# Sixteen of the 384 densely computed tokens go to the gathered side, and the one-hots are made in a new order

## The chip, the cores and the metric

One core of one Trainium2 chip runs one launch of the kernel. The metric is the device time of that launch in microseconds. Engines are named as in the profile: PE is TensorE (matmuls), PEld its weight loads, DVE is VectorE, ACT is ScalarE, POOL is GpSimd, SP is SyncE, which only issues transfers.

## The reference

A decoder layer for 512 tokens of width 2048, all in f32: a modulated norm, one projection, eight heads of differential attention beside four heads of an mLSTM, an output projection, then the PEER layer and a last modulated norm. The change touches the PEER layer only:

```
q = (ht @ w_pq).reshape(T, PEER_HEADS, 2, PEER_QDIM // 2)      # 8 heads
s = jnp.einsum('thcd,hcnd->thcn', q, sub_keys)                 # 128 keys a side
s_top, i_top = lax.top_k(s, PEER_TOPK)                         # 16
...
idx = jnp.take_along_axis(cand_idx, pos, axis=-1)              # one of 128 x 128 experts
g = jax.nn.softmax(sc, axis=-1)
...
u_sel = jnp.take(peer_u, idx_b, axis=0)
a = jax.nn.gelu(jnp.einsum('td,thkd->thk', h_b, u_sel), approximate=False)
w = g_b * a
v_sel = jnp.take(peer_v, idx_b, axis=0)
return jnp.einsum('thk,thkd->td', w, v_sel)
```

So each token uses 8 x 16 = 128 of the 16384 experts; an expert is a row of `peer_u` and a row of `peer_v`, 2048 numbers each.

## The kernel before

The activations stand transposed, features on the partitions, tokens along the free dimension. The PEER layer is computed in two ways. For the first 384 tokens (`TD`) all 16384 experts are multiplied densely, and a table of gates, zero for experts that a token did not choose, weights the results. For the last 128 tokens the chosen rows are gathered from memory: one gather (`gather_load`) fetches one row for each of the 128 tokens, 1 MB, and `gather_use` takes it on VectorE. The rows of `peer_u` are multiplied with `h2row` and summed into one gate column `ga`; the rows of `peer_v` are added with that weight into the same tile. There are 128 gathers of `u` and 128 of `v`, in two buffers `gb`.

An f32 product on TensorE is made of three matmuls of rounded halves (`mm3`, L109 to L111: high by high, high by low, low by high). The halves come from `split`: ScalarE copies the high part (`wh`, L118), VectorE subtracts the low part (`wl`, L119). `s_pump` keeps the splits one tile ahead of their use.

The order of the work is that of the code on each engine; a wait of one instruction holds those behind it.

1. Routing. While VectorE works through the top-k (about 1020 to 1240 us), TensorE is fed with halves of u slices: a u slice is 128 experts times 384 tokens, 48 matmuls; `lead_half` computes half of one, 24 matmuls into `ps_ax`. The first 36 slices (72 halves) are made ahead of the dense stage and stored (`leadd`).
2. The loop of the gate table (about 1250 to 1580 us). `g_hot` makes, for 4 tokens, one-hots of the chosen keys: `ohj` and `ohe` by comparison on VectorE, `ohi` by products with the gates, `ohd` as a reordered copy of `ohj` on ScalarE. `g_mm` multiplies them in 12 bf16 matmuls (L1325) and ScalarE copies the result to `Gs`. Each turn has two `g_hot`, one `lead_half`, in every second turn a gather, the two `g_mm` of the turn before, and one split. 384 tokens make 96 `g_hot`, 48 turns. Behind the loop the rest of the 72 halves follows.
3. The dense stage, 256 steps. Each step takes a tile of `peer_v` (`vr`, split by ScalarE into `hh` at L1442 and by VectorE or POOL into `hl` at L1443), multiplies it with the weighted gates `Wh`, `Wl` in 24 matmuls (`ps_mm`), and adds the sum to `yT`. In steps 0 to 62 that is all TensorE does, since the u slices are ready (`ga` is loaded back); there POOL makes every second `hl`. In steps 63 to 246 a u half, 24 more matmuls (`ps_ax`), follows in each step. `w_slice` multiplies a slice with its gates `g` every second step. The gathers come at half a one a step in steps 0 to 62, then at `rate` a step.
4. The last nine steps and the final norm.

Of the kernel before, what the change touches and what calls it, by code (L numbers as in the profile page):

```python
# [19 lines left out]
P = 128  # L20
T = 512
# [15 lines left out]
TD = ND * P  # L37
# [5 lines left out]
NTG = TD // TG  # L43
# [38 lines left out]
def hymba_layer(ctx: ExitStack, tc: tile.TileContext, I, out: bass.AP):  # L82
# [15 lines left out]
    iota = consts.tile([P, P], F32, name="iota")  # L98
# [25 lines left out]
    items, st = [], {"ld": 0, "sp": 0, "use": 0, "la": 2, "pool": wsp, "auto": False}  # L124
# [372 lines left out]
    nc.sync.dma_start(iota, I["tabs"][:, T_IOTA : T_IOTA + P])  # L497
# [760 lines left out]
    s3 = slice(TD, T)  # L1258
# [5 lines left out]
    y3 = h2row  # L1264
    ijgs = []
# [30 lines left out]
    def g_hot(n):  # L1296


        j, tt = divmod(n * NHOT, P)

        def bc(m):
            return ijgs[j][:, m, tt : tt + NHOT].unsqueeze(1).to_broadcast([P, NK, NHOT])

# [11 lines left out]
        return n, ohd, ohi

    def g_mm(n, ohd, ohi):
        nonlocal Gs
# [74 lines left out]
    yT = yp.tile([P, KT, TD], F32, name="yT")  # L1393
# [19 lines left out]
    def w_slice(i):  # L1413
# [33 lines left out]
    rate = (2 * TR - gk - 0.5 * n_slow) / (NST - NVC - 10 - n_slow)  # L1447
# [5 lines left out]
    def out_gathered(part):  # L1453
        nonlocal x3, sqacc, xr4, y33, pb3
        if part == 0:
            x3 = gbp.tile([P, KT, P], F32, tag="gb", name="x3")
            xr4 = gbp.tile([P, KT, P], F32, tag="gb", name="xr4")
            nc.sync.dma_start(xr4, x1d[:, :, TD:T])
# [10 lines left out]
        elif part == 3:  # L1469
# [4 lines left out]
            nc.vector.tensor_tensor(sqacc[:, TD:T], xr4[:, 0, :], xr4[:, 1, :], op=ALU.add)  # L1474
        elif part == 4:
            pc = bank("ax")
            nc.tensor.matmul(pc[:, 0:1], sqacc[:, TD:T], ones[:, 0:1], start=True, stop=True)
            y33 = rsqrt(mp, pc[:, 0:1], 1, D, "rs3")
# [3 lines left out]
        elif part == 6:  # L1482
# [3 lines left out]
            rb3 = mp.tile([P, P], F32, name="rb3", bufs=1)  # L1486
# [7 lines left out]
    def x_load2(n, tag):
        xt = mp.tile([P, 4, TD], F32, tag=tag, name="xr3")
        nc.sync.dma_start(xt, x1d[:, 4 * n : 4 * n + 4, 0:TD])
        for r in range(4):
            xrs[4 * n + r] = xt[:, r, :]
# [23 lines left out]
    for st_ in range(NST):  # L1522
# [83 lines left out]
    for kt in range(KT):  # L1606
# [6 lines left out]
        nc.sync.dma_start(out[kt * P : (kt + 1) * P, 0:TD], y)  # L1613
# [98 lines left out]
```

## Time and profile before

| | before |
|---|---|
| median of 3 runs | 3489.81 us (3489.24 to 3491.09) |
| the profiled execution | 3489.59 us |
| its span | 3487.8 us |
| PE busy | 3334.1 us, 96% |
| DVE busy | 2713.0 us, 78% |
| ACT busy | 1197.2 us, 34% |
| POOL busy | 626.5 us, 18% |

All times of the trace count from the start of the span; the 1.8 us between span and time lie around it. A share of busy time is a mean over stages that have different limits, so the stages are read one by one.

### The profile page before, as it was taken

How to read it: one execution, taken by the hardware profiler on the slowest of the kernel's cores; microseconds unless marked ns; L12 is line 12 of the kernel's file. 1: busy time of each engine (PE TensorE's matmuls, PEld its weight loads, DVE VectorE, ACT ScalarE, POOL GpSimd, SP SyncE). 2: the span in 40 equal slices, each digit the busy share in tenths (PEclk: the TensorE clock that was granted, in tenths of full speed). 3: DMA queues.
4: the chain of work that ended last, by engine and by line, in shares of the span. 5: the costliest groups of instructions: out<-in, count | busy, mean ns of one | idle time of the engine just before them, and what ended most of it. 6: DMA issues, size and time to landing. Idle time of an engine off the chain costs nothing.

```text
span 3487.8 us, 47774 instructions
## 1 busy us (share of the span) xinstructions
PE 3334.1 (96%) x18323; PEld 3056.8 (88%) x18323; DVE 2713.0 (78%) x4460; ACT 1197.2 (34%) x1747; POOL 626.5 (18%) x408
## 2 busy tenths in 40 slices
PE   8799999999899988889999999999999999999996
PEld 5577777788778877778999999999999999999996
DVE  7968688887669987886777777777777777777777
ACT  3223343333232356664332222323232323232333
POOL 0000123200023410102442111111111111111104
PEclk9999999999999999999999999999999999999998
DMA  8766666769722356778887778787778787877753
GB/s 305 269 232 209 209 216 209 230 225 316 243 91 91 105 171 234 243 242 294 294 303 276 281 276 296 277 285 283 279 279 289 272 294 273 299 278 277 283 189 127
DMA packets 256165, 858.44 MB, mean 246 GB/s; under 512 B 23233, under 2 KB 90433, under 8 KB 223041
## 3 DMA queue, kind: packets, MB, share of 16 engines
q1 hardware_dynamic: 219074, 586.94, 48.8%
q0 software_dynamic: 36864, 268.45, 21.5%
q8 instruction: 144, 2.36, 0.3%
q14 instruction: 83, 0.68, 0.1%
HBM read 810.48 MB, written 40.63 MB: 244 GB/s over the span
## 4 chain that ended last, share of the span: by engine, by line
PE 73%; DVE 17%; ACT 5%; issue 2%; DMA 1%; POOL 0%; SPq 0%; ACTq 0%; POOLq 0%; DVEq 0%
PE ps_mm L109 16%; PE ps_mm L111 16%; PE ps_mm L110 16%; PE ps_ax L109 7%; PE ps_ax L110 7%; PE ps_ax L111 7%; DVE wl L119 3%; ACT Gs L1328 2%; DVE ada L208 2%; ACT wh L118 1%; DVE ohi L1311 1%; PE ps_ax L826 1%; DVE ohj L1308 1%; DVE oh L1151 1%; DVE ohe L1310 1%
## 5 line engine op out<-in xcount | busy, mean ns | idle before, releaser
L119 DVE TENSOR_TENSOR wl<-wr,wh 128x1024 fp32r<-128x1024 f32 (+1 forms) x378 | 472.6, 1251 | 418.0 <-ACT wh L118 415.3
L111 PE MATMUL ps_ax<-hh,wl 128*128 128x384 f32 (+1 forms) x2112 | 717.3, 340 | 31.3 <-DVE wl L119 27.6
L109 PE MATMUL ps_ax<-hh,wh 128*128 128x384 f32 (+1 forms) x2112 | 718.5, 340 | 28.1 <-ACT wh L118 14.8
L110 PE MATMUL ps_ax<-hl,wh 128*128 128x384 f32 (+1 forms) x2112 | 712.7, 337 | 0.0
L109 PE MATMUL ps_mm<-Wh,hh 128*128 128x384 f32 x2048 | 685.6, 335 | 7.9 <-ACT Wh L1421 7.9
L111 PE MATMUL ps_mm<-Wh,hl 128*128 128x384 f32 x2048 | 685.6, 335 | 3.9 <-DVE hl L1443 2.0
L110 PE MATMUL ps_mm<-Wl,hh 128*128 128x384 f32 x2048 | 685.2, 335 | 0.1
L118 ACT CAST wh<-wr 128x1024 fp32r<-128x1024 f32 (+1 forms) x418 | 437.4, 1047 | 525.8 <-PE ps_ax L110 291.1
L111 PEld LDWEIGHTS ps_ax<-hh,wl 128*128 128x128 f32 x2112 | 398.9, 189 | 48.7 <-DVE wl L119 41.4
L109 PEld LDWEIGHTS ps_ax<-hh,wh 128*128 128x128 f32 x2112 | 398.9, 189 | 38.9 <-ACT wh L118 23.8
L110 PEld LDWEIGHTS ps_ax<-hl,wh 128*128 128x128 f32 x2112 | 398.9, 189 | 3.0
L109 PEld LDWEIGHTS ps_mm<-Wh,hh 128*128 128x128 f32 x2048 | 384.9, 188 | 8.5 <-ACT Wh L1421 8.5
L111 PEld LDWEIGHTS ps_mm<-Wh,hl 128*128 128x128 f32 x2048 | 384.7, 188 | 5.7 <-POOL hl L1443 3.2
L110 PEld LDWEIGHTS ps_mm<-Wl,hh 128*128 128x128 f32 x2048 | 385.0, 188 | 0.7 <-DVE Wl L1422 0.7
L109 PE MATMUL ps_mm<-hh,wh 128*128 128x512 f32 x832 | 336.9, 405 | 18.5 <-ACT hh L397 14.8
L110 PE MATMUL ps_mm<-hl,wh 128*128 128x512 f32 x832 | 332.5, 400 | 3.5 <-DVE hl L398 3.5
L111 PE MATMUL ps_mm<-hh,wl 128*128 128x512 f32 x832 | 330.7, 398 | 0.0
L1366 DVE SCALAR_TENSOR_TENSOR h2row<-gb,ga,h2row 128x2048 f32<-128x2048 f32 x127 | 298.0, 2346 | 25.9 <-DMA gb<-in_vN_dram,gx 25.3
L1442 ACT CAST hh<-vr 128x1024 fp32r<-128x1024 f32 x256 | 268.9, 1051 | 127.8 <-PE ps_mm L110 118.6
L1443 DVE TENSOR_TENSOR hl<-vr,hh 128x1024 fp32r<-128x1024 f32 x223 | 279.2, 1253 | 28.5 <-ACT hh L1442 28.5
L1357 DVE SCALAR_TENSOR_TENSOR gb<-gb,h2row 128x2048 f32<-128x2048 f32 x128 | 291.8, 2284 | 11.6 <-DMA gb<-in_uN_dram,gx 11.6
L1344 POOL DMA_INDIRECT gb<-in_vN_dram,gx x128 | 152.9, 1194 | 779.0 <-PE ps_mm L109 347.6
(324 smaller groups left out, 4279.7 us busy)
## 6 DMA issues: line engine op xcount, KB each, us to landing
wr<-in_uT_dram SPq DMA_DIRECT2D x256, 512.0 KB, 5.8
vr<-in_vB_dram SPq DMA_DIRECT2D x256, 512.0 KB, 6.8
wr<-in_adaT_dram SPq DMA_DIRECT2D x192, 512.0 KB, 5.0
ada<-in_adaT_dram SPq DMA_DIRECT2D x66, 512.0 KB, 5.7
wr<-in_winN_dram SPq DMA_DIRECT2D x48, 512.0 KB, 5.2
gd<-Gs SPq DMA_DIRECT2D x12, 2048.0 KB, 8.4
g<-gd SPq DMA_DIRECT2D x32, 768.0 KB, 7.1
wr<-in_winT_dram SPq DMA_DIRECT2D x32, 512.0 KB, 5.2
```

The lines of the kernel that those rows point to most:

```text
L109: ins = nc.tensor.matmul(ps, wh, xh, start=first, stop=False)
L110: nc.tensor.matmul(ps, wh, xl, start=False, stop=False)
L111: nc.tensor.matmul(ps, wl, xh, start=False, stop=last)
L118: nc.scalar.copy(hi, raw)
L119: (lo_eng or nc.vector).tensor_tensor(lo, raw, hi.bitcast(F32), op=ALU.subtract)
L208: nc.vector.scalar_tensor_tensor(w, w, 1.0, cs[:, q * (D // 2) : (q + 1) * (D // 2)], op0=ALU.mult, op1=ALU.mult, accum_out=modr[:, q, col ...
L1328: nc.scalar.copy(Gs[:, :, t0 : t0 + NHOT].rearrange("p i t -> p t i"), pgk.rearrange("p (t i) -> p t i", t=NHOT))
L1344: ins = nc.gpsimd.indirect_dma_start(out=buf.rearrange("p k c -> p (k c)"), out_offset=None, in_=I["uN"] if k < TR else I["vN"], in_offset ...
L1357: nc.vector.scalar_tensor_tensor(buf, buf, 1.0, h2row, op0=ALU.mult, op1=ALU.mult, accum_out=ga3[:, c : c + 1])
L1366: nc.vector.scalar_tensor_tensor(y3, buf, ga3[:, c : c + 1], y3, op0=ALU.mult, op1=ALU.add)
L1442: nc.scalar.copy(hi, raw)
L1443: (nc.gpsimd if few and i % 2 else nc.vector).tensor_tensor(lo, raw, hi.bitcast(F32), op=ALU.subtract)
```

## The change

- `TD` becomes 368. The 16 tokens 368 to 383 are computed by gathers like the last 128: one more gather fetches 8 experts of each of the 16 tokens, 128 rows again, so 16 gathers of `u` and 16 of `v` are added (`gxe`, `gae`, `h2e`; `NE` is 16). All dense matmuls have 368 columns for 384. The loop of the gate table has 92 `g_hot`, 46 turns.
- The row numbers and gates of the 16 tokens are laid out by a store and eight small loads (`ged`, `gef`); the tokens' activations, repeated eight times, are summed (`h3e`) and transposed into `h2e`. At the end 16 matmuls with a 0/1 matrix `sel` add the eight parts of each token into `yT`.
- The transposes of the 128 gathered tokens (`h2row`) move ahead of those for the one-hots (`ijgs`).
- In the loop `g_hot` is split in two: both `ohj` (with `ohd`) first, then the low part of the split that the turn before left (`s_lows`), then `ohe` and `ohi` of both.
- Room is made by fewer buffers: `vr` two for three, `la` one for two. Some tiles of the end take other tags.

```diff
-TD = ND * P
+TY = ND * P
+TE = 16
+TD = TY - TE
+NR = P // TE
...
-        (lo_eng or nc.vector).tensor_tensor(lo, raw, hi.bitcast(F32), op=ALU.subtract)
+        if st["later"] is None:
+            (lo_eng or nc.vector).tensor_tensor(lo, raw, hi.bitcast(F32), op=ALU.subtract)
+        else:
+            st["later"].append((lo_eng or nc.vector, lo, raw, hi))
...
+    def s_lows():
+        while st["later"]:
+            eng, lo, raw, hi = st["later"].pop(0)
+            eng.tensor_tensor(lo, raw, hi.bitcast(F32), op=ALU.subtract)
...
-            lead["la"] = pkl.tile([P, TD], F32, tag="la", name="la", bufs=2)
+            lead["la"] = pkl.tile([P, TD], F32, tag="la", name="la", bufs=1)
...
+    h3e = pk.tile([P, 2 * PH, NK], F32, tag="skt", name="h3e", bufs=1)
+    nc.vector.tensor_tensor(
+        h3e.rearrange("p k (r t) -> p k r t", t=TE),
+        hh.bitcast(F32)[:, :, TD:TY].unsqueeze(2).to_broadcast([P, KT, NR, TE]),
+        hl.bitcast(F32)[:, :, TD:TY].unsqueeze(2).to_broadcast([P, KT, NR, TE]), op=ALU.add,
+    )
+    for r in range(NR):
+        nc.sync.dma_start(gef[r * TE : (r + 1) * TE], ged[:, :, r * NE : (r + 1) * NE])
...
+    NGA = 2 * (TR + NE)
+    def gather_of(k):
+        n, c = divmod(k, TR + NE)
+        return (n, gx, ga3, gw3, c) if c < TR else (n, gxe, gae, gef[:, 1, :], c - TR)
...
     for n in range(0, NG, 2):
-        new = [g_hot(n), g_hot(n + 1)]
+        ohds = [g_hot1(n), g_hot1(n + 1)]
+        s_lows()
+        new = [g_hot2(n, ohds[0]), g_hot2(n + 1, ohds[1])]
...
         hot = new
+        st["later"] = []
         s_pump(1)
...
-            vraw[i] = mp.tile([P, JB * VC], F32, tag="vr", name="vr", bufs=3)
+            vraw[i] = mp.tile([P, JB * VC], F32, tag="vr", name="vr", bufs=2)
...
-    rate = (2 * TR - gk - 0.5 * n_slow) / (NST - NVC - 10 - n_slow)
+    rate = (NGA - gk - 0.5 * n_slow) / (NST - NVC - 11 - n_slow)
...
+            for kt in range(KT):
+                nc.tensor.matmul(pe[:, kt * TE : (kt + 1) * TE], h2e[:, kt, :], sel, start=True, stop=True)
+            nc.scalar.copy(yT[:, :, TD:TY], pe[:, 0 : KT * TE].rearrange("p (k t) -> p k t", t=TE))
```

VectorE, one turn of the loop of the gate table with a gather in it, before (`ib` holds the key numbers, `ijg` the chosen keys and gates):

```order
L119 TENSOR_TENSOR wl<-wr,wh 128x1024
L1308 TENSOR_TENSOR ohj<-ib,ijg_10030 128x512
L1310 TENSOR_TENSOR ohe<-ib,ijg_10030 128x512
L1311 TENSOR_TENSOR ohi<-ohe,ijg_10030 128x1536
L1308 TENSOR_TENSOR ohj<-ib,ijg_10030 128x512
L1310 TENSOR_TENSOR ohe<-ib,ijg_10030 128x512
L1311 TENSOR_TENSOR ohi<-ohe,ijg_10030 128x1536
```

The same engine and place in the changed kernel:

```order
L1347 TENSOR_TENSOR ohj<-ib,ijg_10068 128x512 x2
L132 TENSOR_TENSOR wl<-wr,wh 128x1024
L1356 TENSOR_TENSOR ohe<-ib,ijg_10068 128x512
L1357 TENSOR_TENSOR ohi<-ohe,ijg_10068 128x1536
L1356 TENSOR_TENSOR ohe<-ib,ijg_10068 128x512
L1357 TENSOR_TENSOR ohi<-ohe,ijg_10068 128x1536
L1415 SCALAR_TENSOR_TENSOR gb,ga_7646<-gb,h2row 128x2048
```

Both `ohj` now stand ahead of `wl`, and `wl` ahead of the four others; the gather's use stays behind them.

VectorE, the start of that loop, before (`rem` and `ijg` lead to the table `ijg`, `h` is the sum of the gathered tokens' halves):

```order
L1262 TENSOR_TENSOR h_10023<-hh,hl 128x2048
L1274 TENSOR_TENSOR rem<-ps_mm,ijg_10030 128x128
L1276 TENSOR_TENSOR rem<-rem,ijg_10030 128x128
L1274 TENSOR_TENSOR rem<-ps_mm,ijg_10041 128x128
L1276 TENSOR_TENSOR rem<-rem,ijg_10041 128x128
L1274 TENSOR_TENSOR rem<-ps_mm,ijg_10052 128x128
L1276 TENSOR_TENSOR rem<-rem,ijg_10052 128x128
L119 TENSOR_TENSOR wl<-wr,wh 128x1024
L1293 CAST ib<-iota 128x512
L1308 TENSOR_TENSOR ohj<-ib,ijg_10030 128x512
```

The same place in the changed kernel:

```order
L1298 TENSOR_REDUCE sel<-ident 128x16
L1308 TENSOR_TENSOR rem<-ps_mm,ijg_10068 128x128
L1310 TENSOR_TENSOR rem<-rem,ijg_10068 128x128
L1308 TENSOR_TENSOR rem<-ps_mm,ijg_10079 128x128
L1310 TENSOR_TENSOR rem<-rem,ijg_10079 128x128
L1308 TENSOR_TENSOR rem<-ps_mm,ijg_10090 128x128
L1310 TENSOR_TENSOR rem<-rem,ijg_10090 128x128
L123 TENSOR_TENSOR wl<-wr,wh 128x1024
L1316 TENSOR_TENSOR h3e<-hh,hl 128x2048
L1328 CAST gxe<-gef 128x16
L1336 CAST ib<-iota 128x512
L1347 TENSOR_TENSOR ohj<-ib,ijg_10068 128x512 x2
```

A second wide sum (`h3e`) and a cast of loaded row numbers (`gxe`) now stand ahead of the first one-hot.

TensorE at the same place, changed kernel (before, the 16 transposes of `h` stood one `lead_half` behind the nine of `If`, `Jf` and `Gf`):

```order
L1282 MATMUL ps_mm<-ident,h_10026 128x128 x16
L1303 MATMUL ps_mm<-ident,If 128x128
L1303 MATMUL ps_mm<-ident,Jf 128x128
L1303 MATMUL ps_mm<-ident,Gf 128x128
L1303 MATMUL ps_mm<-ident,If 128x128
L1303 MATMUL ps_mm<-ident,Jf 128x128
L1303 MATMUL ps_mm<-ident,Gf 128x128
```

The transposes of `h` moved ahead of the nine; 16 more, of `h3e`, stand one `lead_half` behind.

## Rows read from the trace of the kernel before

**Rows 1.** Stretches: length, busy us of five engines, clock, DMA share, GB/s.

```profile
1020.00:1240.00 220.00, 203.58 (x1002) 177.79 (x1002) 215.05 (x962) 64.45 (x84) 86.12 (x36) 0.97 0.29 94
...
1250.00:1580.00 330.00, 286.70 (x2271) 258.53 (x2269) 262.70 (x378) 203.22 (x259) 31.79 (x24) 1.00 0.70 236
...
1640.00:1860.00 220.00, 220.00 (x1270) 220.00 (x1268) 168.78 (x237) 69.54 (x80) 103.91 (x52) 1.00 0.84 302
1880.00:3390.00 1510.00, 1510.00 (x8719) 1509.93 (x8718) 1145.79 (x1201) 445.20 (x545) 237.34 (x201) 1.00 0.78 278
```

**Rows 2.** Waits, 1250 to 1580 us: total us, times, longest.

```profile
ACT ohd L1309 <- DVE ohj L1308: 125.0, 93, 1.6
```

**Rows 3.** Timeline of VectorE, two turns: start, us, instruction, idle before.

```profile
1338.62 1.22 DVE L119 TENSOR_TENSOR wl<-wr,wh 128x1024 fp32r<-128x1024 f32 x1 [2.56 <-ACT wh L118]
...
1343.15 2.29 DVE L1357 SCALAR_TENSOR_TENSOR gb<-gb,h2row 128x2048 f32<-128x2048 f32 x1
...
1352.65 1.22 DVE L119 TENSOR_TENSOR wl<-wr,wh 128x1024 fp32r<-128x1024 f32 x1 [2.55 <-ACT wh L118]
```

**Rows 4.** Timeline of ScalarE in the same turns.

```profile
1341.93 0.65 ACT L1309 COPY ohd<-ohj 128x512 bf16<-128x512 bf16 x1 [1.05 <-DVE ohj L1308]
...
1344.36 1.09 ACT L118 CAST wh<-wr 128x1024 fp32r<-128x1024 f32 x1
```

**Rows 5.** Timeline of TensorE, a turn without a wait.

```profile
1256.54 1.53 PE L1325 MATMUL ps_mm<-ohd,ohi 128*128 128x128 bf16 x24
...
1262.13 0.36 PE L1325 MATMUL ps_mm<-ohd,ohi 128*128 128x128 bf16 x3
```

**Rows 6.** Timeline of TensorE: matmuls 1 and 7 of 384, 1 and 5 of 512.

```profile
1999.73 0.33 PE L111 MATMUL ps_mm<-Wh,hl 128*128 128x384 f32 x1
...
2000.77 0.33 PE L111 MATMUL ps_ax<-hh,wl 128*128 128x384 f32 x1
...
600.24 0.40 PE L110 MATMUL ps_mm<-hl,wh 128*128 128x512 f32 x1
...
601.17 0.40 PE L111 MATMUL ps_mm<-hh,wl 128*128 128x512 f32 x1
```

**Rows 7.** Timelines of VectorE and ScalarE at the loop's start.

```profile
1240.43 2.28 DVE L1262 TENSOR_TENSOR h<-hh,hl 128x2048 f32<-128x2048 f32 x1
...
1248.13 2.04 ACT L1285 COPY h2row<-ps_mm 128x512 f32<-128x512 f32 x4
```

**Rows 8.** Lead steps: ScalarE, SyncE's issues; landings at 1707, all gathers.

```profile
1700.68 1.05 ACT L1442 CAST hh<-vr 128x1024 fp32r<-128x1024 f32 x1 [0.83 <-PE ps_mm L110]
...
1709.03 1.05 ACT L1442 CAST hh<-vr 128x1024 fp32r<-128x1024 f32 x1 [0.87 <-PE ps_mm L110]
...
1704.93 0.33 SPq L1429 DMA_DIRECT2D vr<-in_vB_dram  x1
...
1707.17 0.33 SPq L1429 DMA_DIRECT2D vr<-in_vB_dram  x1
...
vr<-in_vB_dram SPq DMA_DIRECT2D x1, 512.0 KB, 7.7
...
gb<-in_uN_dram,gx POOLq DMA_INDIRECT x26, 8.6
```

**Rows 9.** Gathers: issue ns (min/median/max); 1880 to 3390 us: landings, VectorE's waits.

```profile
L1344 POOL DMA_INDIRECT gb<-in_vN_dram,gx x128: 932/937/2917, 2420.9 to 3342.3; - x128
...
gb<-in_vN_dram,gx POOLq DMA_INDIRECT x128, 6.6
gb<-in_uN_dram,gx POOLq DMA_INDIRECT x73, 6.7
...
DVE h2row L1366 <- DMA gb<-in_vN_dram,gx: 25.3, 12, 3.5
DVE gb L1357 <- DMA gb<-in_uN_dram,gx: 11.6, 5, 2.5
```

**Rows 10.** Timeline of TensorE, eight one-column matmuls.

```profile
944.68 1.84 PE L196 MATMUL ps_ax<-ones,sqacc 128*128 128x1 f32 x8 [5.01 <-DVE sqacc L1003]
```

More of the change, by code (lines that the diff above doesn't have):

```diff
@@ L42 @@
 TG = 32
-NTG = TD // TG
+NTG = TY // TG
 NLEAD = 36
@@ L1264, in hymba_layer @@
     y3 = h2row
+    for q in range(4):
+        pw = bank("mm")
+        for r in range(4):
+            nc.tensor.transpose(pw[:, r * P : (r + 1) * P], h3[:, 4 * q + r, :], ident)
+        nc.scalar.copy(h2row[:, 4 * q : 4 * q + 4, :], pw.rearrange("p (k c) -> p k c", k=4))
+    NE = PH * TK // NR
+    geq = pk.tile([P, 2, P], F32, tag="t16", name="geq")
+    nc.vector.scalar_tensor_tensor(
+        geq[:, 0, :], If[:, j3 - 1, :], float(NK), Jf[:, j3 - 1, :], op0=ALU.mult, op1=ALU.add
+    )
+    nc.vector.tensor_copy(geq[:, 1, :], Gf[:, j3 - 1, :])
+    ged = dram.tile([TE, 2, P], F32, name="ged")
+    nc.sync.dma_start(ged, geq[P - TE : P])
+    h2e = gep.tile([P, KT, P], F32, tag="h2e", name="h2e")
+    gef = gep.tile([P, 2, NE], F32, name="gef")
+    gxe = gep.tile([P, NE], I32, name="gxe")
+    gae = gep.tile([P, NE], F32, name="gae")
+    sel = gep.tile([P, TE], F32, name="sel")
+    nc.vector.reduce_sum(sel, ident.rearrange("p (r t) -> p t r", t=TE), axis=AX.X)
     ijgs = []
@@ L1283, in hymba_layer @@
         for r in range(4):
-            nc.tensor.transpose(pw[:, r * P : (r + 1) * P], h3[:, 4 * q + r, :], ident)
-        nc.scalar.copy(h2row[:, 4 * q : 4 * q + 4, :], pw.rearrange("p (k c) -> p k c", k=4))
+            nc.tensor.transpose(pw[:, r * P : (r + 1) * P], h3e[:, 4 * q + r, :], ident)
+        nc.scalar.copy(h2e[:, 4 * q : 4 * q + 4, :], pw.rearrange("p (k c) -> p k c", k=4))
+    nc.vector.tensor_copy(gxe, gef[:, 0, :])
     sK.close()
@@ L1337, in hymba_layer @@
     TR = PH * TK
+    NGA = 2 * (TR + NE)
+    NG = TD // NHOT
     gbuf = {}
+    def gather_of(k):
+        n, c = divmod(k, TR + NE)
+        return (n, gx, ga3, gw3, c) if c < TR else (n, gxe, gae, gef[:, 1, :], c - TR)
     def gather_load(k, after):
         buf = gbp.tile([P, KT, P], F32, tag="gb", name="gb")
+        n, rows, _, _, c = gather_of(k)
         ins = nc.gpsimd.indirect_dma_start(
-            out=buf.rearrange("p k c -> p (k c)"), out_offset=None, in_=I["uN"] if k < TR else I["vN"],
-            in_offset=bass.IndirectOffsetOnAxis(ap=gx[:, k % TR : k % TR + 1], axis=0),
+            out=buf.rearrange("p k c -> p (k c)"), out_offset=None, in_=I["vN"] if n else I["uN"],
+            in_offset=bass.IndirectOffsetOnAxis(ap=rows[:, c : c + 1], axis=0),
         )
@@ L1383, in hymba_layer @@
         hot = new
+        st["later"] = []
         s_pump(1)
+    s_lows()
+    st["later"] = None
     for x in hot:
@@ L1490, in out_gathered, with x_load2 @@
             nc.gpsimd.tensor_tensor(x3, x3, wide(mods("sh_o")), op=ALU.add)
-    xrs, sq = {}, None
[L1494 to L1498, printed above, removed]
+        elif part == 7:
+            pe = bank("ax")
+            for kt in range(KT):
+                nc.tensor.matmul(pe[:, kt * TE : (kt + 1) * TE], h2e[:, kt, :], sel, start=True, stop=True)
+            nc.scalar.copy(yT[:, :, TD:TY], pe[:, 0 : KT * TE].rearrange("p (k t) -> p k t", t=TE))
+    xrs, sq = {}, None
+    def x_load2(pool, tag, k0, n):
+        xt = pool.tile([P, n, TY], F32, tag=tag, name="xr3")
+        nc.sync.dma_start(xt, x1d[:, k0 : k0 + n, 0:TY])
+        for r in range(n):
+            xrs[k0 + r] = xt[:, r, :]
     w_tiles(0)
@@ L1585, in hymba_layer @@
         gnew = []
-        if gk < 2 * TR:
+        if gk < NGA:
             gdue += 0.5 if st_ < n_slow else rate
-            while gdue >= 1.0 and gk < 2 * TR:
+            while gdue >= 1.0 and gk < NGA:
                 gather_load(gk, first)
@@ L1612, in hymba_layer @@
             nc.scalar.activation(y, y, AF.Identity, bias=mod("sh_o", kt), scale=mod("sc_o", kt))
-        nc.sync.dma_start(out[kt * P : (kt + 1) * P, 0:TD], y)
+        nc.sync.dma_start(out[kt * P : (kt + 1) * P, 0:TY], y)
     sO.close()
```

86 lines of the change are left out of this document (47 added, 39 removed).

## The prediction

> **What bounds the kernel now.** TensorE is busy 96% of the span (the table above), so a gain must be work of its own or lie in a stretch where it waits. The table of stretches, read first, says where that is [rows 1]. From 1640 to 3390 us TensorE is busy every microsecond at full granted clock: there only the number and the width of its matmuls count, as long as the others keep up (VectorE is at 169 of 220 us and 1146 of 1510 us, the DMA engines at 84% and 78%). From 1250 to 1580 us (the loop that builds the gate table) TensorE has 43 us idle of 330, and no engine is full.
>
> That loop is read from the chain of its waits. ScalarE waits 125 us for the one-hot `ohj`, 93 times [rows 2]. One turn runs so: `wh` is copied, VectorE subtracts `wl` only after it, then makes `ohj`, `ohe`, `ohi`, and only then the second `ohj`; ScalarE waits for it, copies `ohd`, then the two gate results `Gs`, and only then the next `wh` [rows 3, 4]. Two turns take 1352.65 − 1338.62 = 14.03 us, 7.02 each, and the only idle time of VectorE in the two is 2.55 us before a `wl` [rows 3]. So its work is (14.03 − 2.55)/2 = 5.74 us a turn, one gather in two turns included. TensorE without a wait needs 1262.13 − 1256.54 = 5.59 us [rows 5].
>
> The pace of matmuls: six steps of 384 columns take 1.04 us, 0.1733 us each, and four of 512 take 0.93 us, 0.2325 us each [rows 6]. Both are 0.45 ns a column, so I price 368 columns at 0.1661 us, 0.0072 us less. [...]
>
> **The change, term by term**, against the profiled run's own 3489.6 us (0.2 us under the median, so the same sum serves for both).
>
> a) Start of the loop. As the two listings of TensorE and VectorE show, the 16 transposes of the gathered tokens now stand ahead of the nine that feed `ijg`, and they need the sum `h`, 2.28 us on VectorE; their four ScalarE copies take 2.04 us [rows 7]. The table `ijg` begins about 3 us later, and before the first one-hot VectorE makes a second sum, `h3e`, 2.28 us, and two small ones. Behind them stand all one-hots, and TensorE has nothing else to do. Estimate +6; bounds +2.3 (only `h3e` shows) and +10 (and the small loads that `gxe` waits for land late).
>
> b) The loop. With both `ohj` ahead of `wl`, ScalarE has its `ohd` work early and no longer holds back `Gs` and the next `wh`; what is left is VectorE's 5.74 us a turn. TensorE, at 5.59 − 24 × 0.0072 = 5.42, is below it. I take 5.85 for joints; bounds 5.74 and, if the order gives nothing, 7.02. There are 46 turns for 48: 46 × 5.85 − 48 × 7.02 = −67.9 (bounds −72.9 and −14.0).
>
> c) Two turns fewer leave two more half slices for the stretch behind the loop: 2 × 24 × 0.1661 = +8.0; the seven that were there get narrower, 7 × 24 × 0.0072 = −1.2. Together +6.8.
>
> d) The first 63 steps of the dense stage (24 matmuls a step, 31.5 pairs). The buffers `vr` go from three to two. A pair takes 1709.03 − 1700.68 = 8.35 us [rows 8]; matmuls alone would take 48 × 0.1661 = 7.97. With three buffers a load has about three steps to land, with two it has two. The `vr` load behind POOL's `hl` goes out 1704.93 − 1700.68 = 4.25 us after its `hh`; the other goes out at 1707.17 and landed after 7.7, at 1714.9 [rows 8] (I put that down to the 1 MB gather of the pair and the first load, which share the DMA engines with it). So the second load lands 1714.9 − 1700.68 = 14.2 us behind the first `hh` of its pair. With two buffers it is needed by the second `hh` of the next pair, which stands at least one step of 24 matmuls, 4.0 us, before the end of that pair, 2P after that first `hh` if P is the time of a pair: 2P − 4.0 ≥ 14.2, P ≥ 9.1. That is the wait that the change adds: ScalarE stands at `hh`, behind it `Wh`; SyncE's queue stands at the next `vr`, behind it the loads `ga` and `g`; TensorE waits for `hh`. 31.5 × (9.1 − 8.35) = +24. Bounds: 7.97 a pair, no wait, −12; and if nothing shifts, 7.7 + 2.4 = 10.1 a pair, +55 (2.4 is `hh`, 1.05 [rows 8], a low part on VectorE, 1.22 as `wl` [rows 3], and 0.1 of joints).
>
> e) The other 193 steps. 184 have 48 matmuls: 8.32 us, narrower 7.97, at most −63.6; nine have 24, −1.6: at most −65. Against it: 32 more gathers, 233 for the 128 + 73 of [rows 9], (288 − 23 − 31.5)/174 = 1.34 for (256 − 24 − 31.5)/175 = 1.15 a step. VectorE's work, 0.759 of 8.32 = 6.31 us a step, grows by 0.196 × 2.29 = 0.45 to 6.76 of 7.97, so its spare time goes from 2.0 to 1.2 us. It waited 17 times, 37 us in all, for gathers that landed late [rows 9]. Steps with two gathers rise from about 25 to 59 (the part of the rate above one, over 175 steps); waits in proportion would be 86 us. I let a fifth of that reach TensorE, 16 us: −49. Bounds 0 and −65.
>
> f) The 16 gathered tokens come back by 16 small matmuls in one step: eight of one column took 1.84 us [rows 10], 0.23 each, so +3.7; bounds 0 (a gap of TensorE takes them) and 3.7. The later end of the gathering lies beside matmuls: 0.
>
> Narrower half slices before the loop bring nothing, since VectorE is the full engine there (215 of 220 us [rows 1]). The split multiply of `w_slice` adds a 16-column instruction every second step on VectorE, inside its spare time.
>
> Sum: 6 − 67.9 + 6.8 + 24 − 49 + 3.7 = −76.4, so 3413.
>
> **Rivals.**
> A: the gathers limit the dense stage. Two buffers `gb` serve a chain of issue 0.95, landing 6.6 [rows 9] and use 2.29 [rows 3]: 9.84 us, where each buffer has 2 × 7.97/1.34 = 11.9 us. A landing above 8.7 us stretches the step. For it: where the DMA engines were at 84% (1640 to 1860), a gather took 8.6 us [rows 8]; after the change a step needs 2.31 + 0.205 = 2.52 MB, at 8.06 us 312 GB/s, and 278 GB/s were a share of 0.78 [rows 1], so the share would be 0.88. Against it: one gather in that other stage came with three loads in its 8.3 us too, and nothing waited. A step of 8.3 us gives 184 × 0.24 = 44 more: 3457. [...]
> B, slower than before: the same chain with landings above 9.5 us. The step is then 1.34 × (L + 3.24)/2; at L = 9.5 it is 8.54, 184 × 0.48 = +88: 3501. The gain is used up at a step of 8.48, L = 9.4. Against it: longer steps lower the load, which shortens L.
> C: the lead stage's chain at 10.1 a pair, +31: 3444.
> D: two buffers cost nothing, 7.97 to 8.35 a pair: 24 to 36 less, about 3383. For it: the loads that land early leave the DMA engines idle 16% of that stage.
> E: the new order brings nothing, since VectorE then meets `wl` behind a `wh` that is late itself: 46 × 7.02 is 54 more, 3467.
> F: matmuls do not get shorter with the columns, which the two widths speak against: the dense part's 49 and 1 of c) are lost, 3463.
>
> **How the numbers follow.** Forecast 0.47 (its own range 3395 to 3432), A 0.15, B 0.08, C 0.08, D 0.14, E 0.05, F 0.03. A measurement of this kernel can tell about 0.2%, 7 us, from no change. All but B lie below 3483 as worked out. B, and two of A, C, E and F at once, make 0.09 slower; the far ends of A and E make 0.03 within 7 us; faster is left with 0.88. The range takes in D, C, A, E and F and leaves out B and the far side of D: 3375 to 3470.
>
> **What would show it.** Loop: `ohj` twice ahead of `wl`, ScalarE's waits for `ohj` gone, VectorE without a gap, a turn near 5.85. Lead stage: `hh` waiting for the DMA of `vr`, a pair near 9.1, TensorE no longer at 220 of 220. Dense stage: 0.166 us a matmul, steps near 8.06, landings of gathers at 7 to 8 us and more waits of VectorE for them. Start: first `ohj` some 6 us further behind the last transposes of the step before. Wrong would make it above all a wait at `gb` in most steps, or no wait at `hh` at all.

## The result and the profile after

| | before | changed |
|---|---|---|
| median, 4 runs each | 3489.96 us | 3392.82 us (3388.18 to 3397.16) |
| ratio | | 0.9722, interval 0.9708 to 0.9737 |
| profiled execution | 3489.59 us | 3390.62 us |

The change takes 97 us away; 76 were forecast. The time lies inside the stated range, 3375 to 3470, and 2 us below the forecast's own, 3395 to 3432. The page of the changed kernel, its span and the busy line:

```profile
span 3388.9 us, 48101 instructions
PE 3255.3 (96%) x18323; PEld 2984.0 (88%) x18323; DVE 2766.0 (82%) x4630; ACT 1188.5 (35%) x1745; POOL 701.2 (21%) x441
```

Its stretches, in the columns of [rows 1], cut at the same places of the program: start of the loop, the loop, lead steps, steps with u halves.

```profile
1240.00:1256.00 16.00, 9.65 (x49) 9.35 (x49) 7.67 (x13) 6.42 (x14) 0.00 (x0) 0.71 0.17 50
1256.00:1530.00 274.00, 269.31 (x2284) 256.91 (x2285) 256.35 (x373) 204.10 (x260) 30.25 (x24) 0.99 0.86 285
...
1600.00:1800.00 200.00, 186.89 (x1057) 179.69 (x1058) 140.76 (x221) 56.12 (x67) 99.20 (x46) 0.98 0.75 276
1800.00:3290.00 1490.00, 1487.73 (x8915) 1486.15 (x8915) 1240.91 (x1384) 449.43 (x556) 321.85 (x243) 1.00 0.85 313
```

The loop is now full: VectorE is busy 256 of 274 us and TensorE 269. The lead steps, full before, now have TensorE idle 13 of 200 us. The last row has TensorE full in spite of more gathers; its 2 us idle are waits for POOL's `hl` in the last lead steps. The timelines give the length of each stretch between the same events; the last column is what the prediction said of it.

| from, to | before | after | change | forecast |
|---|---|---|---|---|
| start of the span, sum `h` | 1240.4 | 1239.9 | −0.5 | 0 |
| sum `h`, first `ohj` | 9.4 | 20.7 | +11.3 | a) +6 |
| first `ohj`, last matmul with `ohd` | 333.8 | 259.5 | −74.3 | b) −67.9 |
| then first matmul with `Wh` | 30.0 | 38.6 | +8.7 | c) +6.8 |
| then `hh` for step 63 | 262.1 | 280.5 | +18.4 | d) +24 |
| then `hh` for step 240 | 1469.9 | 1413.6 | −56.3 | e) |
| then last matmul with `Wh` | 117.2 | 111.0 | −6.3 | e) and f): with the row above −45 |
| then the end | 25.0 | 25.1 | +0.1 | 0 |

VectorE in the loop, answering [rows 3]:

```profile
1379.52 1.22 DVE L132 TENSOR_TENSOR wl<-wr,wh 128x1024 fp32r<-128x1024 f32 x1
...
1390.13 0.75 DVE L1347 TENSOR_TENSOR ohj<-ib,ijg 128x512 bf16<-128x512 bf16 x2
1390.80 1.22 DVE L132 TENSOR_TENSOR wl<-wr,wh 128x1024 fp32r<-128x1024 f32 x1
```

There is no gap, and both `ohj` stand ahead of `wl`. From one `wl` to the one two turns later are 11.28 us, 5.64 a turn. ScalarE's wait for `ohj` [rows 2], in the changed loop:

```profile
ACT ohd L1348 <- DVE ohj L1347: 45.0, 23, 2.5
```

45 us, a third of before: ScalarE now waits once in two turns, while VectorE uses the gather, and has time for it.

The start, TensorE and then VectorE, answering [rows 7]:

```profile
1242.27 3.68 PE L1282 MATMUL ps_mm<-ident,h 128*128 128x128 f32 x16 [14.22 <-DVE h L1276]
...
1256.49 3.65 PE L1326 MATMUL ps_mm<-ident,h3e 128*128 128x128 f32 x16 [4.56 <-DVE gxe L1328]
...
1254.06 2.28 DVE L1316 TENSOR_TENSOR h3e<-hh,hl 128x2048 f32<-128x2048 f32 x1
...
1260.17 0.43 DVE L1336 CAST ib<-iota 128x512 bf16<-128x512 f32 x1 [3.74 <-PE ps_mm L1326]
1260.63 0.76 DVE L1347 TENSOR_TENSOR ohj<-ib,ijg 128x512 bf16<-128x512 bf16 x2
```

The first 16 transposes take 3.68 us: TensorE had waited 14 us, and the clock granted to it from 1242.2 to 1246.0 us was 0.50 (mean 0.71 in the whole stretch). Before, the same 16 stood behind a half slice, and the granted clock was 1.00 (1246.4 to 1248.4 us):

```profile
1246.46 1.91 PE L1284 MATMUL ps_mm<-ident,h 128*128 128x128 f32 x16
```

The second 16 stand behind `h3e`. The table `ib` waits 3.74 us for them, since its tile takes the place of `h3e`; that wait was not in the prediction.

The lead steps, answering [rows 8]: ScalarE's wait for the loads (1600 to 1800 us), two `hh` a pair apart, the load between them, and POOL's `hl`:

```profile
ACT hh L1504 <- DMA vr<-in_vB_dram: 81.9, 21, 5.8
...
1700.45 1.05 ACT L1504 CAST hh<-vr 128x1024 fp32r<-128x1024 f32 x1 [3.48 <-DMA vr<-in_vB_dram]
...
1708.99 1.05 ACT L1504 CAST hh<-vr 128x1024 fp32r<-128x1024 f32 x1 [4.02 <-DMA vr<-in_vB_dram]
...
1702.78 0.33 SPq L1491 DMA_DIRECT2D vr<-in_vB_dram  x1
...
1686.47 3.97 POOL L1505 TENSOR_TENSOR hl<-vr,hh 128x1024 fp32r<-128x1024 f32 x1 [5.50 <-ACT hh L1504]
...
1697.05 2.40 POOL L1505 TENSOR_TENSOR hl<-vr,hh 128x1024 fp32r<-128x1024 f32 x1 [5.50 <-ACT hh L1504]
```

The `hh` whose low part VectorE makes now waits for the transfer of `vr` in 26 of 31 pairs. With two buffers the load for the next `hh` of that kind goes out only when this low part is done: here it ends at 1702.76 us and the load goes out at 1702.78. Over 22 pairs a pair takes 9.08 us: on the mean the load goes out 2.34 us after the `hh`, and the next `hh` starts 6.69 us after the load. (A second profile of this kernel, f0 below, has 8.98.)

The steps with u halves, VectorE's waits as in [rows 9]:

```profile
DVE h2row L1424 <- DMA gb<-in_vN_dram,gx: 66.6, 51, 3.3
...
DVE gb L1415 <- DMA gb<-in_uN_dram,gx: 35.2, 28, 3.6
```

79 waits and 102 us for 17 and 37, and with those for the 32 further gathers (14 waits, 22 us) 93 and 124. TensorE feels none of it.

### The profile page after: what moved, and what is told of

Read it like the earlier page. It is cut to its first block, busy times and chain, and to the rows that moved or that the text cites. A ratio compares the mean times of both kernels' runs of the same rounds, so it can differ in the third digit from the quotient of the medians.

```text
span 3388.9 us, 48101 instructions
## 1 busy us (share of the span) xinstructions
PE 3255.3 (96%) x18323; PEld 2984.0 (88%) x18323; DVE 2766.0 (82%) x4630; ACT 1188.5 (35%) x1745; POOL 701.2 (21%) x441
## 4 chain that ended last, share of the span: by engine, by line
PE 65%; DVE 21%; DMA 5%; issue 4%; POOL 3%; ACT 2%; SPq 0%; DVEq 0%; POOLq 0%; ACTq 0%
PE ps_mm L114 13%; PE ps_mm L112 13%; PE ps_mm L113 13%; PE ps_ax L112 7%; PE ps_ax L113 7%; PE ps_ax L114 7%; POOL hl L1505 2%; DMA wr<-in_adaT_dram 2%; DVE ada L220 2%; DVE wl L123 2%; DVE ohi L1357 2%; DVE wl L132 1%; DVE gb L1415 1%; PE ps_ax L837 1%; DMA wr<-in_woutT_dram 1%
## 5 line engine op out<-in xcount | busy, mean ns | idle before, releaser
L112 PE MATMUL ps_ax<-hh,wh 128*128 128x368 f32 (+1 forms) x2112 | 706.1, 334 | 16.0 <-DVE mlqk L481 11.8
L114 PE MATMUL ps_ax<-hh,wl 128*128 128x368 f32 (+1 forms) x2112 | 703.5, 333 | 8.5 <-POOL wl L123 3.8
L113 PE MATMUL ps_ax<-hl,wh 128*128 128x368 f32 (+1 forms) x2112 | 701.8, 332 | 0.0
L114 PE MATMUL ps_mm<-Wh,hl 128*128 128x368 f32 x2048 | 681.0, 333 | 17.9 <-POOL hl L1505 16.4
L112 PE MATMUL ps_mm<-Wh,hh 128*128 128x368 f32 x2048 | 679.1, 332 | 2.0 <-DVE yT L1632 1.6
L113 PE MATMUL ps_mm<-Wl,hh 128*128 128x368 f32 x2048 | 672.8, 329 | 0.1
L123 DVE TENSOR_TENSOR wl<-wr,wh 128x1024 fp32r<-128x1024 f32 (+1 forms) x332 | 416.3, 1255 | 144.4 <-ACT wh L121 140.9
L1400 POOL DMA_INDIRECT gb<-in_uN_dram,gx x128 | 162.1, 1267 | 621.3 <-DVE ohi L1357 171.3
```

The costliest lines, as they stand in the source:

```text
L112: ins = nc.tensor.matmul(ps, wh, xh, start=first, stop=False)
L113: nc.tensor.matmul(ps, wh, xl, start=False, stop=False)
L114: nc.tensor.matmul(ps, wl, xh, start=False, stop=last)
L1400: ins = nc.gpsimd.indirect_dma_start(out=buf.rearrange("p k c -> p (k c)"), out_offset=None, in_=I["vN"] if n else I["uN"], in_offset=bass ...
```

## The experiments

The times of the kernel before on the same chips were 3488.8 to 3491.3 us (medians).

**The order alone** (e1). The diff's lines on `s_lows`, `g_hot1` and `g_hot2` in the kernel before, and nothing else.

> The kernel before with the new order of one-hots alone (384 columns, 48 turns, three vr buffers, no further gathers). Theory: the order alone frees ScalarE, so a turn falls from 7.00 us to VectorE's own 5.65 to 5.75 us, 48 turns give back 60 to 65 us, and the time is 3425 to 3430 us. Rival: the turn fell only because its matmuls got narrower and fewer; then the order alone leaves 7.0 us a turn and 3490 us.

3426.2 us, ratio 0.9815 (0.9799 to 0.9832). VectorE's `wl`, two turns apart:

```profile
1335.94 1.22 DVE L129 TENSOR_TENSOR wl<-wr,wh 128x1024 fp32r<-128x1024 f32 x1
...
1347.22 1.22 DVE L129 TENSOR_TENSOR wl<-wr,wh 128x1024 fp32r<-128x1024 f32 x1
```

11.28 us for two turns, as in the changed kernel, with 384 columns and 48 turns. The order alone brings 65 us; all the rest, on top of it, brings the other 32 of the 97.

**Low part at once** (e2).

```diff
         hot = new
-        st["later"] = []
         s_pump(1)
-    s_lows()
-    st["later"] = None
```

> The changed kernel with both ohj still first, but the low part wl made at once at the end of the turn before, ahead of them. Theory: moving the second ohj forward is most of the gain; the ring wh 1.12, wl 1.14, ohj 0.45, two ohd 1.2, two Gs 1.88 is 5.8 us, and 6.3 on the mean where a gather's turn takes 6.8, against 5.64 now: 7 to 30 us slower than the changed kernel, 3400 to 3423. Rival: it is the deferred wl that frees the turn; then the turn goes back to 7.0 us and the time to about 3455.

3432.4 us, 40 more than the changed kernel; in the profiles 34 of them lie in the loop (293.7 us for 259.5). VectorE:

```profile
1390.54 1.22 DVE L123 TENSOR_TENSOR wl<-wr,wh 128x1024 fp32r<-128x1024 f32 x1
1391.67 0.75 DVE L1347 TENSOR_TENSOR ohj<-ib,ijg 128x512 bf16<-128x512 bf16 x2
...
1396.59 1.23 DVE L123 TENSOR_TENSOR wl<-wr,wh 128x1024 fp32r<-128x1024 f32 x1 [1.43 <-ACT wh L121]
...
1403.34 1.22 DVE L123 TENSOR_TENSOR wl<-wr,wh 128x1024 fp32r<-128x1024 f32 x1
```

Two turns take 12.80 us: `wl` waits again for `wh` in the turn without a gather, and `ohj` behind it. So 7.0 us fell to 6.4 by the moved `ohj` and from there to 5.64 by the deferred `wl`. Both hypotheses named half of it; the expected upper end of 30 us was too low.

**Two `vr` buffers in the kernel before** (e3).

```diff
-            vraw[i] = mp.tile([P, JB * VC], F32, tag="vr", name="vr", bufs=3)
+            vraw[i] = mp.tile([P, JB * VC], F32, tag="vr", name="vr", bufs=2)
```

> The kernel before with two vr buffers for three, nothing else. Theory: in the lead steps the load that goes out behind the second split lands 14.2 us behind the first hh of its pair, so 2P - 4.16 = 14.2 and a pair takes 9.2 us for 8.35; 31.5 pairs are 26 us more, 3516, and the steps with u halves stay at 8.32. Rival: the longer pair of the changed kernel has another cause (moved gathers, narrower tiles); then the time stays at 3490.

3504.4 us, ratio 1.0037 (1.0023 to 1.0051). The stretches of [rows 1] that answer to lead steps and steps with u halves:

```profile
1640.00:1860.00 220.00, 210.22 (x1188) 205.49 (x1189) 158.16 (x222) 64.16 (x75) 109.68 (x51) 1.00 0.77 282
1880.00:3390.00 1510.00, 1509.52 (x8711) 1509.16 (x8711) 1149.17 (x1199) 445.18 (x545) 241.89 (x204) 1.00 0.79 280
```

The place is right: TensorE loses 10 of 220 us in the lead steps and nothing later. The size is not: a pair takes 8.84 us, the stretch to step 63 is 16 us longer (278.1 for 262.1), where 26 were expected.

**`hl` on VectorE** (e4) and **gathers one step later** (e8), each in the changed kernel.

```diff
-            few = i < NLEAD * 2 - AHEAD or i >= NH + 5
+            few = i >= NH + 5
```

> The changed kernel with every hl of the lead steps on VectorE, none on POOL. Theory: POOL's 3.05 us stands in the chain from hh to the next vr load; with VectorE's 1.22 the loads go out 1.8 us earlier, 2P - 4.0 = 12.4, a pair takes 8.2 for 9.1 and the time falls by 28 us to 3365. Rival: the transfers or VectorE (1.2 us more work in a pair) limit the pair, and the time stays at 3393 or rises.

```diff
-    gdue, gnew = 0.0, []
+    gdue, gnew = 0.5, []
```

> The changed kernel with the gathers of the lead steps one step later (the count that paces them starts at 0.5 instead of 0), so that a gather goes out in the step of VectorE's hl and no longer right behind POOL's. Theory: the gather that goes out 1 us behind the first vr load makes the second land late; moved away from it, both loads land sooner, the pair falls from 9.08 to 8.0 to 8.4 us and the time by 21 to 34 us to 3359 to 3372. Rival: the chain is that of POOL's hl and the two loads alone, or the gather hurts as much where it goes; then the time stays at 3390 to 3396.

3389.6 and 3393.8 us, pairs of 8.72 and 8.80: both theories failed, and the times are near those of their rivals. The stretch to step 63 is 9 and 4.5 us shorter than in f0 (270.8 and 275.2 us for 279.7). VectorE and SyncE in e4:

```profile
1692.09 2.28 DVE L1415 SCALAR_TENSOR_TENSOR gb<-gb,h2row 128x2048 f32<-128x2048 f32 x1
...
1694.31 0.98 DVE L1632 TENSOR_TENSOR yT<-yT,ps_mm 128x368 f32<-128x368 f32 x2
1695.20 1.22 DVE L1505 TENSOR_TENSOR hl<-vr,hh 128x1024 fp32r<-128x1024 f32 x1
...
1696.45 2.65 SPq L1491 DMA_DIRECT2D vr<-in_vB_dram  x2
```

`hh` had begun at 1692.43. On POOL `hl` started 0.1 us behind the end of `hh` (1697.05 us for 1696.97 in the changed kernel); on VectorE it stands behind the use of a gather and `yT`, and the load goes out 4.02 us after `hh`. On the mean of 22 pairs that is 4.40 us, against 4.54 in the changed kernel: the edit did not do what it was meant to do. In e8 the gather's use stood ahead of VectorE's own `hl`:

```profile
1695.96 3.33 DVE L1415 SCALAR_TENSOR_TENSOR gb<-gb,h2row 128x2048 f32<-128x2048 f32 x1 [0.78 <-DMA gb<-in_uN_dram,gx]
...
1698.23 1.06 ACT L1504 CAST hh<-vr 128x1024 fp32r<-128x1024 f32 x1 [3.57 <-DMA vr<-in_vB_dram]
```

The use takes 3.33 us, for 2.28 in the row of e4, and `hh` waits 3.57 us for its load, as before. So neither says what a pair would be with earlier loads; that the gather's transfer as such delays the second load is not shown.

**The start** (e5). Both sums go to POOL, the `ijg` transposes come first again, `h3e` lies in a gather buffer, and its transposes come in the second turn.

```diff
-    nc.vector.tensor_tensor(h3, hh.bitcast(F32)[:, :, s3], hl.bitcast(F32)[:, :, s3], op=ALU.add)
+    nc.gpsimd.tensor_tensor(h3, hh.bitcast(F32)[:, :, s3], hl.bitcast(F32)[:, :, s3], op=ALU.add)
...
-    h3e = pk.tile([P, 2 * PH, NK], F32, tag="skt", name="h3e", bufs=1)
-    nc.vector.tensor_tensor(
+    h3e = gbp.tile([P, KT, P], F32, tag="gb", name="gb")
+    nc.gpsimd.tensor_tensor(
...
         first = lead_half()
+        if n == 2:
+            for q in range(4):
+                pw = bank("mm")
+                for r in range(4):
+                    nc.tensor.transpose(pw[:, r * P : (r + 1) * P], h3e[:, 4 * q + r, :], ident)
+                nc.scalar.copy(h2e[:, 4 * q : 4 * q + 4, :], pw.rearrange("p (k c) -> p k c", k=4))
```

> The changed kernel with another start of the loop: the transposes for ijg ahead of those of h as before, both wide sums h and h3e on POOL, h3e in a gather buffer, and its 16 transposes in the loop's second turn. Theory: the first ohj stands 20.7 us behind the sum h in the changed kernel and 9.4 before, because of 16 transposes at the low clock, h3e, and ib that waits for the second 16; with this start it comes about 10 us earlier and the time falls by 8 to 11 us to 3382 to 3385. Rival: the sums take so long on POOL, or slow VectorE so much, that less than 4 us come back.

3388.7 us (3377.3 to 3393.0). In its place the gain is there: the first `ohj` at 1249.73 us for 1260.63, the loop's last matmul 11.1 us earlier. In the total it is only 4 us, which the spread of the times doesn't separate from none: the steps with u halves, which the edit doesn't touch, give 8 us back (1288.5 us for 160 steps against 1280.2; see the last section).

**The gathers' density** (e6, e9): the rate times 1.25 and 1.1.

```diff
-    rate = (NGA - gk - 0.5 * n_slow) / (NST - NVC - 11 - n_slow)
+    rate = 1.25 * (NGA - gk - 0.5 * n_slow) / (NST - NVC - 11 - n_slow)
```

> The changed kernel with its gathers 1.25 times as dense from step 63 on (1.68 a step in place of 1.34), so that they end some 35 steps earlier; same work. Theory of the two buffers: a step takes at least 1.68 x (6.6 + 3.24)/2 = 8.3 us with landings as before, 0.3 more over 139 steps, 40 us in all, 3433, and more where landings get longer. Rival: there is still room, VectorE has 6.3 + 0.53 x 2.29 = 7.5 us of 7.97 to do; then the time stays within 6 us of 3393.

3592.3 us, 200 more, far beyond both. A stretch of it, and VectorE's waits:

```profile
2200.00:2400.00 200.00, 177.93 (x1001) 174.49 (x1000) 159.62 (x188) 50.84 (x65) 47.65 (x36) 0.95 0.83 306
...
DVE h2row L1424 <- DMA gb<-in_vN_dram,gx: 130.1, 71, 4.6
DVE gb L1415 <- DMA gb<-in_uN_dram,gx: 79.3, 39, 5.9
```

A step takes 9.57 us (steps 80 to 200), one gather in 9.57/1.677 = 5.70 us; the changed kernel has one in 5.96. DMA is less busy than in the changed kernel (0.83 for the 0.88 of its row below), VectorE has a fifth of its time free. That leaves the two buffers; the next run has the parts of their round.

> The changed kernel with its gathers 1.1 times as dense from step 63 on (1.476 a step). With 1.677 a step a step took 9.57 us, one gather in 5.70 us, against one in 5.96 us now. Theory: 5.7 us a gather is what the two buffers give, so a step takes 1.476 x 5.70 = 8.4 us over some 158 steps and the time rises by 65 us to about 3460. Rival: the stretch at 1.677 comes from steps with two gathers in a row that hold VectorE back; at 1.476 they are still apart often enough, and the time rises by less than 25 us, to under 3420.

3468.5 us, 76 more than the changed kernel. A step takes 8.41 us, and 8.41/1.476 is 5.70 us a gather again, as the limit says. TensorE in steps with u halves, and the landings from 1880 to 3200 us, as in [rows 9]:

```profile
2200.00:2700.00 500.00, 483.04 (x2831) 477.92 (x2830) 418.43 (x445) 141.38 (x179) 111.13 (x88) 0.99 0.87 320
...
gb<-in_vN_dram,gx POOLq DMA_INDIRECT x128, 7.3
```

TensorE is idle 17 of 500 us, where the changed kernel has none. Over 175 gathers (2000 to 3000 us) one round of a buffer is, on the mean, 1.28 us of issue, 6.08 from its end to the landing, 1.07 until VectorE comes to it, 2.32 of use and 0.68 to the next issue: 11.43 us, 5.7 for each of two buffers. In the kernel before the third of these parts was 4.60 us; that was the room. No run had a third buffer, so the limit is read from this sum and from the two equal paces.

**Without the further gathers** (e7): `NGA = 2 * TR`, the other 32 gathers left out.

> The changed kernel without the 32 further gathers (the 16 tokens get no experts; their layout, sum and the 16 small matmuls stay), rate 1.16 a step. Theory: the gathers cost almost nothing, since a step takes 8.00 us with them and its matmuls 7.97: 2 to 7 us less, 3386 to 3391. Rival of the prediction: a fifth of VectorE's 102 us of waits reaches TensorE, then some 16 to 20 us less, 3375.

3405.2 us, 12 more with less work; the two profiled executions are 20 apart. A stretch of it and VectorE near the end; then the same stretch of the changed kernel:

```profile
2000.00:2200.00 200.00, 200.00 (x1194) 200.00 (x1193) 157.80 (x195) 60.24 (x75) 35.39 (x30) 1.00 0.81 294
...
3335.88 9.34 DVE L1505 TENSOR_TENSOR hl<-vr,hh 128x1024 fp32r<-128x1024 f32 x2 [5.08 <-ACT hh L1504]
3345.14 3.57 DVE L1481 TENSOR_TENSOR ga<-ga,g 128x16 f32<-128x16 f32 x1
```

```profile
2000.00:2200.00 200.00, 200.00 (x1202) 200.00 (x1201) 167.41 (x205) 60.90 (x76) 40.60 (x34) 1.00 0.88 325
```

TensorE is full in both, so the 32 gathers cost it no wait. But it does 1194 matmuls here and 1202 there in 200 us; that is 8 us over 160 steps. Another 11 us are at the end (from step 240 on 121.9 us for 111.0), where TensorE waits 7.2 us for `Wh`; the next section comes back to it.

**The changed kernel again, with more buffers, and with both mends** (f0, f1, f2; one chip). f1 gives the lead steps four buffers:

```diff
-            vraw[i] = mp.tile([P, JB * VC], F32, tag="vr", name="vr", bufs=2)
+            if 2 <= i < 60:
+                vraw[i] = wrawp.tile([P, W1], F32, tag="wraw", name="wr")
+            else:
+                vraw[i] = mp.tile([P, JB * VC], F32, tag="vr", name="vr", bufs=2)
...
+        if st_ == 59:
+            st["cap"] = 1 << 30
+            s_pump(1)
```

> The changed kernel itself, so that the next two are compared with it on one chip. The steps with u halves take 8.000 us in its first profile and 8.054 in the profiles of two experiments that left them alone, all without a wait of TensorE. Theory: the spacing of the 368-column matmuls falls into one of two patterns from execution to execution, so the single times of this kernel spread over some 9 us (160 steps x 0.054), 3388 to 3398. Rival: the pattern belongs to a kernel, then this one stays within 3 us of one value.

> The changed kernel with four vr buffers in lead steps 2 to 59: they take the buffers wr, which hold the raw u tiles and are idle there; the loads of u ahead of their use wait until step 59. Theory: the two vr buffers alone make the pair 9.08 us; with four no hh waits for a load, the pair falls to TensorE's 8.0 to 8.1 and the time by 28 to 33 us to 3360 to 3365. Rival: POOL's hl of 3.4 us or the transfers limit the pair as well; then it stays above 8.6 and less than 15 us come back.

> The same with the other start of the loop as well (both wide sums on POOL, the ijg transposes first). Theory: the two gains lie in different stretches and add, 28 to 33 and 11 us: 3349 to 3354. Rival: the earlier start is given back in the stretch behind the loop, then 3360 to 3365 as without it.

Medians of five: 3395.9 (3386.3 to 3401.6), 3374.9 and 3361.1 us. The lead steps of f1:

```profile
1600.00:1800.00 200.00, 199.76 (x1172) 195.94 (x1171) 155.38 (x244) 63.80 (x74) 98.60 (x50) 1.00 0.84 305
...
1690.32 1.05 ACT L1507 CAST hh<-wr 128x1024 fp32r<-128x1024 f32 x1 [3.00 <-PE ps_mm L113]
...
1698.35 1.05 ACT L1507 CAST hh<-wr 128x1024 fp32r<-128x1024 f32 x1 [2.94 <-PE ps_mm L113]
```

No `hh` waits for a load, TensorE is full, a pair takes 8.18 us, and the stretch to step 63 falls from 279.7 to 255.9 us. So POOL's `hl` and the transfers do not limit the pair; the number of buffers does. The total gains 21 us where 28 were the least expected; in the profiles 6 us are lost in the steps with u halves (1288.0 us for 160 steps against 1281.6). f2 adds 14 to that by the medians; its ratio to the kernel before is 0.9630 (0.9615 to 0.9645), below the interval of f1 (0.9655 to 0.9682). Its profiled execution is the slowest of its five (3371.4 us; they reach down to 3355.4): the gain at the start of the loop is there, 11.5 us, but the routing ahead of it, which neither edit touches, ended 8 us later than in f1's.

## Why the prediction was right, point by point

The mechanism of the largest term, b), was right: e1 shows that the order alone empties VectorE's gap, and VectorE's own work, 5.64 us measured for 5.74 worked out and 5.85 taken, is the turn. The stretch gained 74.3 us, 1.4 more than the sum's own bound. Rival E is refuted.

a) was mis-sized: 11.3 us, beyond its upper bound of 10. Two things were missing, `ib` waiting for the place of `h3e` (3.7 us), and transposes at a granted clock of 0.50 behind TensorE's wait of 14 us, 3.68 us for 1.91 (the work for `ijg` comes 5 us later, where 3 were said). e5 took 11 us back there.

c) is 2 us larger than the sum. 1.6 of them are three waits of TensorE for `wl` behind the loop, of which the kernel before has none there.

d) The mechanism stands where it was put, `hh` waiting for `vr`, and f1 shows the buffers to be the cause. That the number agrees, 9.08 us a pair for 9.1, is luck. The sum held two lengths fixed that both moved, and the two errors cancel: from the first `hh` of a pair to the second load there are 7.4 us for its 6.5, and from that load to the `hh` that needs it 6.7 for its 7.7. (POOL's `hl`, 3.05 us before, takes 2.40 to 3.97 after the change, which the sum did not have either.) The same sum gave 9.2 for e3, which took 8.84. The stage cost 18 and not 24 us. Rivals C and D, 10.1 and no wait, are out.

e) was mis-sized most: 16 us of waits were to reach TensorE, and none did. The two rows of the table that hold e) and f) gave 62.6 for 45: 16 us are these waits, 5 go the other way, since a matmul of 368 columns takes 0.1667 us and not 0.1661, and 6 come from the end, below. e7 shows that they cost nothing: TensorE is full with the 32 gathers and without them. Rivals A and B did not come, but e6 and e9 show how near they were: 10% denser gathers cost 76 us. Their mechanism, two buffers in a chain, fits. Their price was low: with landings of 6.6 us the chain gives one gather in 4.92 us and e6 a step of 8.3, where 5.70 and 9.57 were measured. A round of 11.43 us in e9 is 1.6 longer than the chain's 9.84. 0.8 of that are longer landings (7.36 us on the mean), 1.1 are the wait of a landed gather for its place in VectorE's order, and 0.7 the way from a use to the next issue; the chain had neither of the last two, but counted the 0.95 of the issue twice, since the profile's landing starts with the issue. With the changed kernel's own 1.34 a step it is 5.96 us a gather against 5.70 at the limit.

f) The small matmuls, and a stretch of TensorE behind them:

```profile
3259.32 4.66 PE L1557 MATMUL ps_ax<-sel,h2e 128*128 128x16 f32 x32
...
3264.00:3268.00 4.00, 4.00 (x14) 4.00 (x15) 1.34 (x2) 1.32 (x2) 0.00 (x0) 0.50 0.42 119
```

They take 4.66 us for 3.7 (32 in the trace for 16 in the code), and behind them the granted clock is 0.50 until 3268.5 us (0.99 from there to 3272, 1.00 from 3250 to 3254): 14 matmuls in 4 us, where 26 went in 3250 to 3254. By these two rates that costs about 2 us more, which the sum did not have. Even so the time from step 240 on is 6.3 us shorter, for a cause that no term of the sum had. Rows of before that were not read for the prediction show what went away; VectorE, POOL, and TensorE's wait near the end:

```profile
3414.76 9.34 DVE L1443 TENSOR_TENSOR hl<-vr,hh 128x1024 fp32r<-128x1024 f32 x2 [5.23 <-ACT hh L1442]
3424.02 3.96 DVE L1418 TENSOR_TENSOR ga<-ga,g 128x384 f32<-128x384 f32 x1
...
3418.54 4.48 POOL L1489 TENSOR_TENSOR x<-x,modc 128x2048 f32<-128x2048 f32 x1
3423.09 4.47 POOL L1490 TENSOR_TENSOR x<-x,modc 128x2048 f32<-128x2048 f32 x1
...
PE ps_mm L109 <- ACT Wh L1421: 7.5, 1, 7.5
```

and VectorE at that place in the changed kernel:

```profile
3314.63 4.75 DVE L1505 TENSOR_TENSOR hl<-vr,hh 128x1024 fp32r<-128x1024 f32 x1
...
3326.00 2.75 DVE L1505 TENSOR_TENSOR hl<-vr,hh 128x1024 fp32r<-128x1024 f32 x2 [4.92 <-ACT hh L1504]
```

POOL runs three instructions of 128x2048 for the final norm, two products and a sum. Beside them VectorE's `hl`, elsewhere 1.22 us, takes 4.7 each and `ga`, 0.55 elsewhere, takes 3.96: it ends 0.4 us after POOL's last instruction (3427.56). TensorE then waited 7.5 us for `Wh`. In the changed kernel POOL's three meet fewer of VectorE's instructions, none of them a slice's `ga`, and TensorE has no such wait. In e7, whose count of gathers is that of before, the collision is back (rows above: 9.34 for two `hl`, 3.57 for a 16-column `ga`), and with it a wait of 7.2 us. No run moved POOL's three alone; the cause is read from these rows. In the rows of before each of VectorE's three starts 0.9 us behind one of POOL's three (which start at 3413.86, 3418.54 and 3423.09 us) and ends 0.4 to 1.1 us behind its end.

F is out: 48 matmuls take 8.00 us for 8.32.

## What to carry to other kernels

When an engine takes its work in the order of the code, as VectorE does here, and mixes work that depends on a late input with work that doesn't, look for the ring through two engines before counting busy time: moving one comparison and deferring one subtraction gave two thirds of this gain (65 of 97 us, e1). When buffers pay for something else, check each stage that uses them at its own step time; here the third buffer was worth nothing in steps of 8 us and 16 us of the stretch with steps of 4 (e3), and four in place of two were worth 24 there (f1). A kernel can be full on TensorE and still stand within a few per cent of another limit: a run with that load raised by a tenth shows it (76 us more in e9).

## What was not expected of the hardware

In the kernel before, the matmuls of 384 columns come evenly, every 172 to 174 ns (2000 to 3200 us). Those of 368 columns come unevenly, 162 to 170 ns apart for the most part in the same stretch of the changed kernel, and over the runs in two patterns, of 8.00 or 8.05 us a step, without any wait of TensorE. The first profile of the changed kernel has the faster one over 160 steps (1280 us), e5, e7 and f2 have the slower one (1288.5 to 1289 us). Over ten steps the matmuls of the v side (`ps_mm`) average 168.7 ns in the slower pattern and 166.5 in the faster, those of the u halves (`ps_ax`) 166.9 in both. The expectation for f0 was that executions of one kernel fall into either. But the pattern can change inside an execution, and in f0 and e8 it does so behind a moment in which TensorE was held: f0 starts with the slower and goes to the faster at 2050 us, behind a spacing of 0.40 us between two matmuls; e8 goes to the slower at 2190 us, behind 0.85 us, and back at 2852, behind 1.14. f0's times spread over 15 us, where the kernel before spreads over 4, and its profile had the faster pattern for the most part at 3394 us, so the pattern is not all of the spread. What sets it was not tried.

POOL's issue of a gather of `peer_v` takes 0.94 us in the median and up to 2.92 in the kernel before [rows 9]; in e6 one of 2.88 us, from 2425.51 us on, overlaps a use of a gather on VectorE, from 2425.22 to 2427.57 us.
